# Hybrid decoder trunk in two layers: ScalarE issues first weights and three kinds of copies, and all blocks of x have rooms of their own

## The chip, the cores and the metric

The kernel runs on one core of one Trainium2 chip. The metric is the device time of one execution in microseconds (us); lower is better. TensorE (PE) multiplies matrices, VectorE (DVE) and ScalarE (ACT) work element by element, GpSimd (POOL) does so on SBUF alone, and SyncE (SP) issues DMA transfers. ScalarE can issue transfers too. Each engine works through its own instructions in order and waits on semaphores.

## The reference, cut to what matters

The input x has 1024 tokens of width 1024; 16 meta tokens are put ahead, so there are 1040 rows. Everything is float32. Each of the two layers computes

```python
u = rms_norm(h, norm_g)
dq, dk, dv, dz, fq, fk, fv, fz, f_logit = split(u @ w_in)    # w_in: 1024 x 4104
# 4 differential heads: two 64-wide query/key halves with rope, values of 128
p  = softmax(q1 k1' / 8) - lam * softmax(q2 k2' / 8)         # causal
o_a = rms_norm(p @ v_a, subln_g) * (1 - lambda_init)
# 8 forgetting heads of 64: cum = cumsum(log_sigmoid(f_logit + b_forget))
o_b = softmax(q_f k_f' / 8 + cum_q - cum_k) @ v_f            # causal
h = h + concat(o_a * silu(dz), o_b * silu(fz)) @ w_out
```

and a final RMS norm drops the meta rows.

## The kernel before, in words

**Split precision.** A float32 product is made of three float32r products: each operand is split into a high part (a rounded copy) and a low part (the rest), and high by high, low by high and high by low are added in PSUM. The normed and transposed input stands in two resident tiles, XTh (high) and XTl (low), with 1040 columns for the tokens.

**The start** (lines 936 to 968, then `prefetch` from line 969). Nine blocks of rows are loaded: block 0 is the 16 meta tokens, blocks 1 to 8 have 128 tokens each. `XORD` (line 38) gives the order of the loads: 1, 0, 2, 3, ..., 8. `htags` (line 944) gives each block a tag, which is a ring of buffers: block 0 and blocks 6 and 7 use "st" (three buffers), blocks 1 to 5 use "e" (four buffers, `NE`), block 8 uses "ot" (two, one of them for the norm's weights gb). With `W0` = 8 (line 39) the first weights, the key columns of unit 0, are loaded by `load_w` behind the ninth block. Then come three groups (`GRPS`, line 42): blocks 0 to 2, 3 to 5, 6 to 8. For each group `rms_stats` squares the blocks on ScalarE (line 256) and works out the inverse root on VectorE (lines 257 and 231 to 244). `rms_apply` makes u (line 267), and `put_ut` transposes it on TensorE (line 282), copies the high part on ScalarE (line 292) and subtracts the low part on VectorE (line 293).

**Weights.** `load_w` (line 296) loads 1024 x 128 weights in four transfers of 128 KB (lines 302 and 308) and splits each on GpSimd (lines 314 and 317). Raw and low parts share the tag "wlo" (six buffers). `prefetch(0, "qv")` (line 982) loads the first query columns into a free V buffer and the value columns of units 0 and 1 together, with the forget logits' columns, by `load_v01` (line 351, splits on lines 369 and 370).

**Units.** A layer has eight units of 128 columns: units 0 to 3 are the differential heads, units 4 to 7 pairs of forgetting (fox) heads. `unit_proj` (line 471) projects keys and queries in three chunks of columns by `proj` (line 333, matmuls on line 341). `CH_ALL` has chunks of 348, 346 and 346 columns, `CH_BLK` of 272, 384 and 384, whose borders are those of blocks. `CKB` is off, so `CH_ALL` is used for keys. In a differential unit the projection is copied out (line 491), its halves are exchanged by four small transfers (line 499), and the rope is worked out on VectorE and GpSimd (lines 500 to 502); then `split_k` and `split_q` make high parts on ScalarE (line 515 or 517) and low parts (line 508 or 510). The high part of the queries is duplicated into the other half of the partitions (line 560, two transfers per chunk or unit). In a fox unit the high keys are also copied (line 533) into a tile of tag "q2" with two buffers, beside rows of cumulated logits. Unit 0 projects the values of units 0 and 1 (`proj_v01`, line 373: meta rows on line 385, blocks on line 406) and the forget logits, which go to DRAM in eight small transfers (line 418). `attend` makes scores (lines 679 and 681), subtracts the maximum (line 685), exponentiates on ScalarE (line 692), transposes the probabilities (lines 854 to 870) and multiplies by the values.

**Order.** The helper `dma` (line 136) issues every transfer on SyncE. The program is written in the order above, but the framework lays out each engine's instructions anew by a simulated timeline (line 1168, `schedule_with_timeline_sim`): what is ready early in the simulation comes early, across stages. On the chip every engine, SyncE's queue too, then keeps its order.

Of the kernel before, what the change touches and what calls it, by code (L numbers as in the profile page):

```python
# [12 lines left out]
F32 = mybir.dt.float32  # L13
# [6 lines left out]
P = 128  # L20
NM = 16
SEQ = 1024
L = NM + SEQ
# [9 lines left out]
ST = 3  # L33
# [5 lines left out]
W0 = 8  # L39
# [34 lines left out]
CKB = False  # L74
# [4 lines left out]
WQ0 = False  # L79
WQ1 = False  # L80
# [33 lines left out]
def hybrid_kernel(ctx: ExitStack, tc: tile.TileContext, x, meta, norm_g, w_in, b_forget,  # L114
# [21 lines left out]
    def dma(dst, src):  # L136
        nc.sync.dma_start(out=f32(dst), in_=f32(src))  # L137

# [157 lines left out]
    def load_w(l, col, q=None, room=None, rawroom=None):  # L296
# [3 lines left out]
        for qt in range(4 if rawroom else 0):  # L300
            raws.append(rawroom(qt))
            (q or nc.sync).dma_start(out=raws[-1], in_=w_in[l, 256 * qt:256 * qt + 256, col:col + P].rearrange("(k p) c -> p k c", p=P))
# [30 lines left out]
    def proj(l, col, chunks, evac):  # L333
        his, los = ahead.pop((l, col), None) or load_w(l, col, nc.scalar if (WQ1 and l == 0 and col % 512 == 0 and col < 2048) else None)
# [38 lines left out]
    def proj_v01(l, his, los):  # L373
# [43 lines left out]
        for h in range(8):  # L417
            dma(fx[h, NM:].rearrange("(b t) -> b t", t=P), ft[8 * h:8 * h + 8])
# [52 lines left out]
    def unit_proj(l, j, U, tabs):  # L471
# [3 lines left out]
        ch_q = CH_ALL if l == 0 else CH_REAL  # L475
# [52 lines left out]
        yield from project(ck, CH_BLK if CKB and l == 0 and j == 0 else CH_ALL, 0, 1.0, split_k)  # L528
        if not diff and KE:
            U.Kb = []  # L530
            for m in range(2):
                k2 = q2t("k2")
                dma(k2[0:64], U.K1[m][halves[m]])
                dma(k2[64:68], augk[:, 2 * (j - 4) + m])
                U.Kb.append(k2[0:68])
# [12 lines left out]
        def split_q(src, c0, scale, t0, n):  # L548
# [10 lines left out]
            for m in range(2):  # L559
                dma(U.Qa[m][halves[1 - m], c], U.Qa[m][halves[m], c])  # L560
# [4 lines left out]
        if not diff and not KE:  # L565
            U.Kb = []
            for m in range(2):
                k2 = q2t("k2")
                dma(k2[0:64], U.K1[m][halves[m]])
# [374 lines left out]
    htags = [("st", ST)] + [("e", NE)] * 5 + [("st", ST)] * 2 + [("ot", OTB)]  # L944
    for i, b in enumerate(XORD):
        t0, n = blk(b)
        tg, nb = htags[b]
        hb = big.tile([P, L], F32, name="hb", tag=tg, bufs=nb or None)[:, :D]
# [5 lines left out]
        if i == W0:  # L954
            ck0 = unit_cols(0)[1]
            ahead[0, ck0] = load_w(0, ck0, nc.scalar if WQ0 else None, None, (lambda qt: wp.tile([P, 2, P], F32, name="wraw", tag="wlo", bufs=WLB or None)) if KR else None)
# [12 lines left out]
    def prefetch(l, todo):  # L969

        for w in todo:
# [3 lines left out]
            if w == "q":  # L975
                room = vp.tile([P, NB, 2, P], F32R, name="wroom", tag="V")
                ahead[l, col] = load_w(l, col, None, room,
                                       lambda qt: slot("es")[:, :256].rearrange("p (k c) -> p k c", k=2))
# [193 lines left out]
```

## Time and profile before

| what | value |
|---|---|
| three runs | 1501.41, 1500.04, 1497.89 us |
| median | 1500.04 us |
| the profiled execution | 1498.74 us |
| its span, first to last instruction | 1497.1 us |
| mean granted TensorE clock | 0.982 of full speed |
| TensorE busy | 1419.0 us, 95% |
| VectorE, ScalarE, GpSimd busy | 64%, 47%, 42% |

Times in the rows are from the span's start. A DMA's row tells when its engine issued it, not when the data moved; what waited for the data tells when it was there. In an idle remark, [25.62 <-DVE u L267] means that the engine stood still for 25.62 us and that VectorE's line 267 ended it. In a queue's row several issues can be merged into one ("x4"), and waiting between them is then inside the duration.

### The profile page before, as it was taken

Reading aid. Unit: us, or ns where it says so; the run is one execution under the profiler, and the core shown is the slowest. Engines: PE = TensorE matmul, PEld = TensorE weight load, DVE = VectorE, ACT = ScalarE, POOL = GpSimd, SP = SyncE. Lnnn points to the kernel's source line nnn. Section 1 sums busy time; section 2 is a strip of 40 time slices with the busy share of each in tenths; the row PEclk is TensorE's granted clock in tenths of the full one; section 3 lists DMA queues with packets and bytes.
Section 4 is the critical chain, followed back from the end, with each engine's and each line's share of the span. In section 5 each row is a group of like instructions: output and inputs, shape, how many; then the busy total and the mean of one; then the engine's idle time right before and its main releaser. Section 6 shows DMA issues by size and latency. Waiting matters only on the chain.

```text
span 1497.1 us, 26781 instructions
## 1 busy us (share of the span) xinstructions
PE 1419.0 (95%) x9262; PEld 1348.8 (90%) x9262; DVE 955.3 (64%) x2721; ACT 699.9 (47%) x1729; POOL 627.8 (42%) x1118
## 2 busy tenths in 40 slices
PE   2889989899999999999999899899999999999997
PEld 2888989899999999997789899899999999999886
DVE  3548695957665656566564498867757555755653
ACT  3335554445454555456222365545445555654521
POOL 3525553633344444565106255435334454445500
PEclk7899999999999999999999999999999999999999
DMA  8314331332234224346434044224242323243632
GB/s 192 56 40 63 50 73 32 82 30 55 59 86 76 52 52 75 73 154 183 103 128 94 20 63 68 47 51 75 34 79 63 79 45 78 61 108 88 220 120 91
DMA packets 112280, 119.63 MB, mean 80 GB/s; under 512 B 15441, under 2 KB 92881, under 8 KB 112145
## 3 DMA queue, kind: packets, MB, share of 16 engines
q1 hardware_dynamic: 112144, 117.93, 36.2%
q8 instruction: 73, 1.20, 0.3%
q14 instruction: 63, 0.51, 0.1%
HBM read 70.92 MB, written 21.54 MB: 62 GB/s over the span
## 4 chain that ended last, share of the span: by engine, by line
PE 75%; DVE 8%; DMA 5%; SPq 4%; ACT 3%; issue 2%; POOL 2%; DVEq 0%; POOLq 0%; ACTq 0%
PE pj L341 36%; PE pss L1059 5%; PE pj L1059 5%; PE pss L679 4%; PE pt L854 4%; PE pss L681 4%; SPq L137 3%; PE pj L406 2%; PE po L788 2%; PE po L789 2%; DMA sw<-raw 2%; DMA wraw<-in_w_in_dram 2%; DVE E L685 2%; PE pt L1059 1%; POOL sw L501 1%
## 5 line engine op out<-in xcount | busy, mean ns | idle before, releaser
L341 PE MATMUL pj<-XTh,whi 128*128 128x346 f32 (+5 forms) x1392 | 454.7, 328 | 7.6 <-POOL whi L314 3.9
L341 PE MATMUL pj<-XTh,wlo 128*128 128x346 f32 (+5 forms) x1392 | 451.2, 325 | 3.6 <-POOL wlo L317 3.5
L341 PE MATMUL pj<-XTl,whi 128*128 128x346 f32 (+5 forms) x1392 | 450.4, 324 | 0.0
L341 PEld LDWEIGHTS pj<-XTh,whi 128*128 128x128 f32 x1392 | 263.0, 189 | 12.2 <-POOL whi L314 5.9
L341 PEld LDWEIGHTS pj<-XTh,wlo 128*128 128x128 f32 x1392 | 263.6, 189 | 6.2 <-POOL wlo L317 5.7
L341 PEld LDWEIGHTS pj<-XTl,whi 128*128 128x128 f32 x1392 | 263.3, 189 | 0.7 <-DVE XTl L293 0.3
L685 DVE CUSTOM_DVE_ANT_0 E<-pss,cst 128x456 f32<-128x456 f32 (+6 forms) x384 | 210.2, 557 | 68.6 <-PE pss L681 42.1
L692 ACT ACTIVATE E<-E,cst 128x400 f32<-128x400 f32 (+2 forms) x192 | 172.4, 898 | 137.2 <-DVE cst L685 130.5
L317 POOL TENSOR_TENSOR wlo<-wraw,whi 128x256 fp32r<-128x256 f32 x232 | 183.3, 790 | 65.7 <-PE pj L341 50.9
L763 DVE TENSOR_TENSOR ptl<-pt,pth 128x512 fp32r<-128x512 f32 (+1 forms) x240 | 150.2, 634 | 54.9 <-ACT pth L762 51.1
L314 POOL TENSOR_SCALAR whi<-wraw 128x256 fp32r<-128x256 f32 x232 | 106.7, 460 | 186.7 <-DMA wraw<-in_w_in_dram 156.6
L762 ACT CAST pth<-pt 128x512 fp32r<-128x512 f32 (+1 forms) x240 | 126.9, 543 | 92.9 <-PE pt L854 34.5
L679 PE MATMUL pss<-k,qa 128*128 128x400 f32 (+7 forms) x448 | 152.4, 345 | 10.0 <-DMA qa<-qa 5.0
L709 POOL TENSOR_SCALAR E<-E,cst 128x400 f32<-128x400 f32 (+2 forms) x96 | 83.8, 874 | 132.3 <-DVE cst L708 102.3
L662 POOL TENSOR_SCALAR XTl<-ql 64x128 fp32r<-64x128 f32 x136 | 50.8, 379 | 120.4 <-PE pss L681 95.6
L679 PEld LDWEIGHTS pss<-k,qa 128*128 128x128 f32 x448 | 85.0, 190 | 15.7 <-DVE cst L685 9.3
L854 PE MATMUL pt<-cst,E 128*128 128x128 f32 x576 | 88.0, 275 | 0.2
L788 PE MATMUL po<-pth,V 128*128 128x256 f32 x320 | 85.0, 286 | 0.0
L789 PE MATMUL po<-ptl,V 128*128 128x256 f32 x320 | 82.8, 287 | 0.0
L501 POOL TENSOR_TENSOR sw<-sw,sin 128x694 f32<-128x694 f32 (+3 forms) x32 | 51.0, 1595 | 57.2 <-DMA sw<-raw 51.4
L681 PE MATMUL pss<-k,XTl 128*128 128x400 f32 (+6 forms) x224 | 72.0, 327 | 0.0
L681 PE MATMUL pss<-k,q 68*128 68x400 f32 (+6 forms) x224 | 71.9, 325 | 0.0
(300 smaller groups left out, 2948.7 us busy)
## 6 DMA issues: line engine op xcount, KB each, us to landing
wraw<-in_w_in_dram SPq DMA_DIRECT2D x248, 128.0 KB
hb<-in_x_dram SPq DMA_DIRECT2D x16, 512.0 KB
wor<-in_w_out_dram SPq DMA_DIRECT2D x64, 128.0 KB
sw<-raw SPq DMA_DIRECT2D x48, 86.8 KB
ms<-OT SPq DMA_DIRECT2D x8, 520.0 KB
k<-k SPq DMA_DIRECT2D x16, 260.0 KB
h<-hb SPq DMA_DIRECT2D x8, 512.0 KB
ms<-OT SPq DMA_DIRECT2D x8, 512.0 KB
```

The lines of the kernel that those rows point to most:

```text
L317: nc.gpsimd.tensor_tensor(out=lo, in0=raw, in1=hi.bitcast(F32), op=ALU.subtract)
L341: nc.tensor.matmul(ps[:, :n], lhsT=w, rhs=xx[:, k, t0:t0 + n], start=(cnt == 0), stop=(cnt == 23))
L679: nc.tensor.matmul(ps[:, :nn], lhsT=U.Qa[m][:, t:t + P], rhs=U.K1[m][:, c0:c0 + nn], start=True, stop=False)
L681: nc.tensor.matmul(ps[:, :nn], lhsT=low[m], rhs=U.Kb[m][:, c0:c0 + nn], start=False, stop=True)
L685: nc.vector.tensor_tensor_reduce(out=E[:, c0:c0 + n], in0=ps[:, :n], in1=k, scale=-1.0, scalar=s[:, c - 1:c] if CHN and c else -NEG, op0=A ...
L692: nc.scalar.activation(E[:, :W], E[:, :W], AF.Exp, scale=-1.0, bias=lo, accum_out=s[:, 4:5])
L762: nc.scalar.copy(hi, ps)
L763: nc.vector.tensor_tensor(out=lo, in0=ps, in1=hi.bitcast(F32), op=ALU.subtract)
L788: nc.tensor.matmul(o[:, :256], lhsT=U.V[:, kb, hd, :], rhs=hi, start=False, stop=False)
L789: nc.tensor.matmul(o[:, :256], lhsT=U.V[:, kb, hd, :], rhs=lo, start=False, stop=last)
L854: nc.tensor.transpose(ps[:, (2 * a + b) * P:(2 * a + b + 1) * P], PP[:, k0:k0 + P], ident)
L1059: nc.tensor.matmul(ps, lhsT=xx[:, k, m0:m0 + P], rhs=wo[k][w][:, c], start=(k == 0 and i == 0), stop=(k == KT - 1 and i == 2))
```

## The change

Five things change. The first weights (keys of unit 0) are loaded right behind the first block of x instead of behind the ninth, and both they and the first query weights are issued by ScalarE, in two transfers of 256 KB into one tile of tag "qa0" or "qa1" instead of four of 128 KB. Block 5 of x gets a buffer of tag "k1" and block 8 one of "k0". Unit 0 uses the chunks `CH_BLK` for its keys in both layers and for its queries in layer 0. The duplicates of queries, the copies of fox keys and the transfers of the forget logits are issued by ScalarE (`dma_a`). The rope's exchanges, the low queries, the rows of logits and all other weights stay with SyncE.

```diff
--- before.py
+++ after.py
@@ -36,7 +36,7 @@
 MW = 584
 AHEAD = 3
 XORD = (1, 0, 2, 3, 4, 5, 6, 7, 8)
-W0 = 8
+W0 = 0
 ON_POOL = ()
 SPL_POOL = ()
 GRPS = ((0, 1, 2), (3, 4, 5), (6, 7, 8))
@@ -71,13 +71,13 @@
 SH = 0
 PP = ()
 WARM = 20
-CKB = False
+CKB = (0,)
 KR = True
 PG = ()
 AQ = True
 AV = True
-WQ0 = False
-WQ1 = False
+WQ0 = True
+WQ1 = True
 CORD = (1, 0, 2, 3)
 PSB = (0, 0, 0, 0)
 Z_AT = {0: [0], 1: [1], 2: [2], 4: [3], 7: [4, 5, 6, 7]}
@@ -135,6 +135,10 @@
 
     def dma(dst, src):
         nc.sync.dma_start(out=f32(dst), in_=f32(src))
+
+    def dma_a(dst, src):
+
+        nc.scalar.dma_start(out=f32(dst), in_=f32(src))
 
     def pj(nm="pj"):
         return ps_j.tile([P, 512], F32, name=nm, tag="pj")
@@ -293,13 +297,20 @@
                 nc.vector.tensor_tensor(out=lv, in0=psv, in1=hv.bitcast(F32), op=ALU.subtract)
 
 
-    def load_w(l, col, q=None, room=None, rawroom=None):
+    def load_w(l, col, q=None, room=None, rawroom=None, rawtag=None):
 
         his, los = [], []
         raws = []
-        for qt in range(4 if rawroom else 0):
-            raws.append(rawroom(qt))
-            (q or nc.sync).dma_start(out=raws[-1], in_=w_in[l, 256 * qt:256 * qt + 256, col:col + P].rearrange("(k p) c -> p k c", p=P))
+        if rawroom == "half":
+
+            whole = stk.tile([P, L], F32, name="wraw4", tag=rawtag, bufs=STB or None)[:, :D].rearrange("p (k c) -> p k c", k=KT)
+            for a in (0, 4):
+                (q or nc.sync).dma_start(out=whole[:, a:a + 4], in_=w_in[l, P * a:P * a + 4 * P, col:col + P].rearrange("(k p) c -> p k c", p=P))
+            raws = [whole[:, 2 * qt:2 * qt + 2] for qt in range(4)]
+        elif rawroom:
+            for qt in range(4):
+                raws.append(rawroom(qt))
+                (q or nc.sync).dma_start(out=raws[-1], in_=w_in[l, 256 * qt:256 * qt + 256, col:col + P].rearrange("(k p) c -> p k c", p=P))
         for qt in range(4):
           if rawroom:
             raw = raws[qt]
@@ -331,7 +342,7 @@
             late.pop(0)()
 
     def proj(l, col, chunks, evac):
-        his, los = ahead.pop((l, col), None) or load_w(l, col, nc.scalar if (WQ1 and l == 0 and col % 512 == 0 and col < 2048) else None)
+        his, los = ahead.pop((l, col), None) or load_w(l, col)
         for t0, n in chunks:
             ps = pj(f"pj_{l}_{col}")
             cnt = 0
@@ -415,7 +426,7 @@
         ft = ptp.tile([P, 256], F32, name="ft", tag="pm")[0:64, 0:P]
         nc.scalar.copy(ft, ps[0:64, 0:P])
         for h in range(8):
-            dma(fx[h, NM:].rearrange("(b t) -> b t", t=P), ft[8 * h:8 * h + 8])
+            dma_a(fx[h, NM:].rearrange("(b t) -> b t", t=P), ft[8 * h:8 * h + 8])
 
 
     def forget(l):
@@ -472,7 +483,7 @@
         diff = j < 4
         cq, ck, cv, _ = unit_cols(j)
         tq = 0 if l == 0 else NM
-        ch_q = CH_ALL if l == 0 else CH_REAL
+        ch_q = (CH_BLK if j in CKB else CH_ALL) if l == 0 else CH_REAL
         U.diff, U.j, U.l, U.tq = diff, j, l, tq
         lowhalf, tophalf = slice(0, 64), slice(64, 128)
         halves = (lowhalf, tophalf)
@@ -525,12 +536,12 @@
                 hi = U.K1[m][halves[m], t0:t0 + n]
                 hi_part(hi, x, scale)
                 sub(U.K1[m][halves[1 - m], t0:t0 + n], x, scale, hi, f'k{m}')
-        yield from project(ck, CH_BLK if CKB and l == 0 and j == 0 else CH_ALL, 0, 1.0, split_k)
+        yield from project(ck, CH_BLK if j in CKB else CH_ALL, 0, 1.0, split_k)
         if not diff and KE:
             U.Kb = []
             for m in range(2):
                 k2 = q2t("k2")
-                dma(k2[0:64], U.K1[m][halves[m]])
+                dma_a(k2[0:64], U.K1[m][halves[m]])
                 dma(k2[64:68], augk[:, 2 * (j - 4) + m])
                 U.Kb.append(k2[0:68])
         U.Qa = [stk.tile([P, L], F32R, name=f"qa{m}") for m in range(2)]
@@ -557,7 +568,7 @@
             c = slice(todo_q[0][0], t0 + n)
             todo_q.clear()
             for m in range(2):
-                dma(U.Qa[m][halves[1 - m], c], U.Qa[m][halves[m], c])
+                dma_a(U.Qa[m][halves[1 - m], c], U.Qa[m][halves[m], c])
             if not diff:
                 for m in range(2):
                     dma(q2s[m][0:64, c], ql[halves[m], c])
@@ -566,7 +577,7 @@
             U.Kb = []
             for m in range(2):
                 k2 = q2t("k2")
-                dma(k2[0:64], U.K1[m][halves[m]])
+                dma_a(k2[0:64], U.K1[m][halves[m]])
                 dma(k2[64:68], augk[:, 2 * (j - 4) + m])
                 U.Kb.append(k2[0:68])
 
@@ -941,11 +952,11 @@
     dma(bfb, bcast_rows(b_forget, P))
     hbs = {}
     gb = None
-    htags = [("st", ST)] + [("e", NE)] * 5 + [("st", ST)] * 2 + [("ot", OTB)]
+    htags = [("st", ST)] + [("e", NE)] * 4 + [("k1", STB)] + [("st", ST)] * 2 + [("k0", STB)]
     for i, b in enumerate(XORD):
         t0, n = blk(b)
         tg, nb = htags[b]
-        hb = big.tile([P, L], F32, name="hb", tag=tg, bufs=nb or None)[:, :D]
+        hb = (stk if tg[0] == "k" else big).tile([P, L], F32, name="hb", tag=tg, bufs=nb or None)[:, :D]
         dma(hb[:n], meta if b == 0 else x2[P * (b - 1):P * b])
         hbs[b] = (hb, n)
         if i == 0:
@@ -953,7 +964,7 @@
             dma(gb, bcast_rows(norm_g[0], P))
         if i == W0:
             ck0 = unit_cols(0)[1]
-            ahead[0, ck0] = load_w(0, ck0, nc.scalar if WQ0 else None, None, (lambda qt: wp.tile([P, 2, P], F32, name="wraw", tag="wlo", bufs=WLB or None)) if KR else None)
+            ahead[0, ck0] = load_w(0, ck0, nc.scalar if WQ0 else None, None, "half", "qa0")
     utags = ("k0", "k1", "qa0", "qa1") * 2 + ("ql",)
     for grp in GRPS:
         us = [stk.tile([P, L], F32, name="u", tag=utags[b])[:, :D] for b in grp]
@@ -974,8 +985,11 @@
                 ahead[l, col] = load_w(l, col)
             if w == "q":
                 room = vp.tile([P, NB, 2, P], F32R, name="wroom", tag="V")
-                ahead[l, col] = load_w(l, col, None, room,
-                                       lambda qt: slot("es")[:, :256].rearrange("p (k c) -> p k c", k=2))
+                if l == 0:
+                    ahead[l, col] = load_w(l, col, nc.scalar if WQ1 else None, room, "half", "qa1")
+                else:
+                    ahead[l, col] = load_w(l, col, None, room,
+                                           lambda qt: slot("es")[:, :256].rearrange("p (k c) -> p k c", k=2))
             if w == "v":
                 ahead[l, "v"] = load_v01(l)
```

## Rows read from the trace of the kernel before

**Rows 1.** The page: busy time by engine; the chain that ended last, by engine.

```profile
PE 1419.0 (95%) x9262; PEld 1348.8 (90%) x9262; DVE 955.3 (64%) x2721; ACT 699.9 (47%) x1729; POOL 627.8 (42%) x1118
...
PE 75%; DVE 8%; DMA 5%; SPq 4%; ACT 3%; issue 2%; POOL 2%; DVEq 0%; POOLq 0%; ACTq 0%
```

**Rows 2.** TensorE's waits, whole span: line, who released it, us in total, times, longest us.

```profile
PE pt L282 <- DVE u L267: 29.0, 3, 25.6
PE pss L799 <- DMA qa<-qa: 5.9, 1, 5.9
PE pss L679 <- DMA qa<-qa: 5.0, 2, 4.8
```

**Rows 3.** Timeline of TensorE, 10 to 88 us: start us, us, instruction [idle before <- releaser].

```profile
13.22 3.61 PE L282 MATMUL pt<-cst,u 128*128 128x128 f32 x16 [0.53 <-DVE u L267]
...
42.45 2.82 PE L282 MATMUL pt<-cst,u 128*128 128x128 f32 x12 [25.62 <-DVE u L267]
...
73.17 0.28 PE L385 MATMUL pj<-vwh,mm 128*48 128x264 f32 x1
...
87.03 0.35 PE L799 MATMUL pss<-k,qa 128*128 128x16 f32 x1 [5.91 <-DMA qa<-qa]
```

**Rows 4.** Timeline of VectorE, 0 to 62 us: the three groups' norms.

```profile
10.69 3.67 DVE L267 SCALAR_TENSOR_TENSOR u<-hb,cst,gb 16x1024 f32<-16x1024 f32 x3
...
20.82 3.81 DVE L267 SCALAR_TENSOR_TENSOR u<-hb,cst,gb 128x1024 f32<-128x1024 f32 x3
...
41.11 4.15 DVE L267 SCALAR_TENSOR_TENSOR u<-hb,cst,gb 128x1024 f32<-128x1024 f32 x3
```

**Rows 5.** Timeline of ScalarE, 0 to 62 us: the eighth and the ninth block's squares.

```profile
15.96 1.06 ACT L256 ACTIVATE u<-hb 128x1024 f32<-128x1024 f32 x1
...
37.75 1.06 ACT L256 ACTIVATE u<-hb 128x1024 f32<-128x1024 f32 x1 [19.19 <-DMA hb<-in_x_dram]
```

**Rows 6.** Timeline of SyncE's queue, 0 to 62 us: DMA issues.

```profile
6.88 4.82 SPq L137 DMA_DIRECT2D gsc<-in_subln_g_dram  x1
11.74 4.72 SPq L302 DMA_DIRECT2D wraw<-in_w_in_dram  x4
16.50 8.72 SPq L302 DMA_DIRECT2D cst<-in_w_in_dram  x4
25.27 0.86 SPq L137 DMA_DIRECT2D cos<-in_rope_cos_dram  x1
...
28.09 2.75 SPq L137 DMA_DIRECT2D bfb<-in_b_forget_dram  x1
30.97 0.61 SPq L137 DMA_DIRECT2D hb<-in_x_dram  x1
```

**Rows 7.** Groups of instructions, shapes apart: a block's low parts, busy us, mean ns.

```profile
L293 DVE TENSOR_TENSOR XTl<-pt,XTh 128x512 fp32r<-128x512 f32 x32 | 21.3, 685 | 10.9 <-ACT XTh L292 10.6
```

**Rows 8.** Timeline of GpSimd, 0 to 75 us: weight splits.

```profile
20.15 0.43 POOL L314 TENSOR_SCALAR whi<-wraw 128x256 fp32r<-128x256 f32 x1 [16.21 <-DMA wraw<-in_w_in_dram]
...
42.57 3.28 POOL L370 TENSOR_TENSOR vwl<-wraw,vwh 128x256 fp32r<-128x256 f32 x2 [3.48 <-DVE u L267]
...
57.58 0.74 POOL L370 TENSOR_TENSOR vwl<-wraw,vwh 128x256 fp32r<-128x256 f32 x1
```

**Rows 9.** Three stretches: length, busy us by engine, granted clock, DMA share, GB/s.

```profile
2.00:14.00 12.00, 7.98 (x52) 7.70 (x53) 5.09 (x14) 7.17 (x16) 1.91 (x8) 0.97 1.00 352
14.00:26.00 12.00, 2.83 (x14) 2.49 (x12) 8.77 (x24) 4.52 (x10) 3.82 (x5) 0.64 0.95 43
26.00:38.00 12.00, 0.00 (x0) 0.00 (x0) 0.00 (x0) 0.25 (x1) 6.49 (x12) 0.50 0.83 202
```

**Rows 10.** DMA issues of the copies: count, ns min/median/max, first and last start us.

```profile
L137 SPq DMA_DIRECT2D qa<-qa x48: 461/500/1239, 83.6 to 1309.3; - x48
...
L137 SPq DMA_DIRECT2D k<-k x16: 461/467/468, 353.9 to 1301.6; - x16
```

**Rows 11.** SyncE's queue, whole span: waits for the scores' second matmul.

```profile
SPq L137 <- PE pss L681: 101.4, 11, 15.7
```

## The prediction

> **What bounds the kernel now.** I read the page's busy times first, then TensorE's waits, then the timelines of the first 110 us engine by engine. TensorE is busy 95% of the span [rows 1], so a change counts only where TensorE stands still, or where it makes TensorE stand still. Its waits name few such places [rows 2]: one of 25.6 us before the transposes of line 282, one of 5.9 us before line 799 and 5.0 us in two waits before line 679, the last three for the copy of query halves (qa<-qa). The reader should see that a third of its idle time, 78 us, is one wait at the start.
>
> That wait is from 16.83 us (13.22 + 3.61), when the transposes of blocks 1, 0 and 2 end, to 42.45 us [rows 3]. VectorE applies the norm three times at 10.69, three times at 20.82 and three times at 41.11 us [rows 4]. ScalarE squares eight blocks up to 17.02 us; the ninth waits 19.19 us for its transfer and comes at 37.75 us [rows 5]. SyncE's queue shows why: one x transfer is issued at 30.97 us, behind gsc, four weight issues of k, four of q (from 16.50), the rope tables and the biases [rows 6]. By the code it is block 5, the fifth tile on a tag with four buffers. Its group (3, 4, 5) comes before (6, 7, 8) in TensorE's order, so the norms finished at 24.63 us lie idle until 42.45 us. From there TensorE is never without work up to 81.12 us: six blocks' transposes and the projections of k and q end at 73.17 us, 30.72 us after 42.45, and the v projection follows [rows 3].
>
> **The change part by part.** The sum is made against the profiled execution, 1498.74 us (span 1497.1 and 1.6 around it), 1.3 below the median of 1500.04.
>
> *Rooms for all x.* Block 5 gets a buffer of k1 and block 8 one of k0; nothing must be freed, so all nine issues stand at the head of SyncE's queue. What is late next is VectorE. Group 0 is applied by 14.36 us. Its subtractions (line 293) take four of 0.685 us [rows 7] and the small meta ones, 3.0 us. Each further group needs its statistics, 2.3 us (ScalarE's square ends at 38.81, the applies start at 41.11 [rows 4, 5]), 3.8 us of applies and six subtractions, 4.1 us: 10.2 us. So the last block is split at 14.4 + 3.0 + 10.2 + 10.2 = 37.8 us.
>
> *First weights in ScalarE's queue, and chunks at block borders.* With a first k chunk of 272 columns TensorE needs only blocks 0 to 2 and can begin at 17.4 us (14.4 + 3.0) instead of after group 1. From there the work that took 30.72 us before ends at 48.1 us, if nothing starves it. By VectorE the bound is much the same: after 37.8 us the last chunk of k and of q remains, 384 of 1040 columns, at most that share of the 30.72 us (which hold transposes too), 11.3 us: 49.1 at most. The v projection then starts at 48.1 instead of 73.17: **25.1 us saved**. The first weights must be split by 17.4 us: issued at 2 to 3 us, they share the engines with x; GpSimd, waiting 16.21 us up to 20.15 [rows 8], splits them in under 5 us. This is hidden.
>
> The price is that 1.05 MB of k and q weights now move among the x transfers. From 2 to 14 us the engines are fully busy at 352 GB/s [rows 9]: more queues cannot move more. At that rate the weights delay x by 3.0 us, at the 43 GB/s of 14 to 26 us (weights among gsc's tiny pieces) by 24 us. I take the row between, 202 GB/s at 0.83 busy, 243 when full, as it too mixes weights and long rows: 4.3 us. The eighth block was read at 15.96 us, so the last of nine is there at 15.96 + 1.5 + 4.3 = 21.8; VectorE turns to its statistics at 27.6, after 3.2 us of squares. So it costs 0, and up to 17.5 us at the slow rate. The Trainium skill ("DMA: Bandwidth & Descriptors", Issuing engines are not separate DMA queues) speaks against this part: a second issuing engine shares the same 16 DMA engines and saves issue time alone. By that rule the queue itself gives no bandwidth, and what is left is the earlier place; the sum above counts only that.
>
> *Weights of v.* Their last split ended at 58.32 us (57.58 + 0.74) [rows 8]; before, TensorE wanted them 15 us later, now it would want them 10 us earlier. SyncE loses the eight issues from 11.74 to 25.2 us (13.4 us), and the wait of 3.48 us behind a late norm goes, so the end can be 41.4 us; the other end is 58.3. I take 45, nearer the first because the issues are gone from that queue by the diff: no cost, at most 10.2 us.
>
> *Copies begun by ScalarE.* Moved from SyncE: 48 query copies of 0.5 us, 16 fox-key copies of 0.47 us [rows 10] and 16 forget-logit transfers, at most as long: 40 us. What an issue holds ScalarE for is not in the trace: 0 to 0.5 us each. The chain has 3% ScalarE, 45 us of its 699.9 busy [rows 1], so 6.4% of its time counts: **2.6 us lost** of 40 (ends 0 and 40). Behind an issue stand the exponentials and PSUM copies of attention, and TensorE's transposes wait for them; mostly it has projection matmuls to do meanwhile. The logits' eight issues per layer stand ahead of attention's first exponentials. SyncE is relieved by the same 40 us, which can shorten the three waits for qa<-qa by 0 to 10.9 us; I take 0, since those copies left SyncE as soon as ScalarE had written the halves, and the wait is mostly the flight. They therefore stay.
>
> *Fox keys.* A copy's room (two buffers) is free only when the unit before has made its last scores. On SyncE such waits for line 681 sum to 101.4 us in 11 [rows 11]. On ScalarE the same wait would hold everything queued behind it. Ends 0 and 101.4; I take 0, as each engine's order is laid out by simulated readiness, so that other ready ScalarE work stands ahead. The chunk borders in layer 1 move no column: 0.
>
> Sum: 1498.74 - 25.1 + 2.6 = 1476.2; beside the median, which lies 1.3 higher, **1477**.
>
> **The rivals.** (1) *The v weights stay late*: v starts at 58.3, saving 14.9 us: 1498.74 - 14.9 + 2.6 = 1486.4. For it: two of them at a time go through two buffers, and the engines are full early. Against: 13.4 us less in the queue ahead. Chance 0.17. (2) *The query waits go too*: 10.9 more: 1465.3, and 1462.7 if ScalarE's issues cost nothing. For it: SyncE's queue is shorter. Against: those waits are flight. Chance 0.09. (3) *ScalarE stands at the key copies*: the 11 waits of 9.2 us move to it, and half reaches TensorE: 1476.2 + 50.7 = 1526.9. It decides the sign once 22.5 us, 2.0 per wait, reach TensorE. Against: the layout by readiness. Chance 0.07. (4) *The order is laid out such that block 5 or the first weights are late again*: the change does not do what it says, 1498.74 + 2.6 = 1501.3. Against: nothing has to be freed for them. Chance 0.05. The forecast, from 1470 to 1484, keeps 0.62.
>
> **How the numbers follow.** The time is that of the forecast. The range goes down to rival 2 (1463) and up over rival 1 with twice ScalarE's cost (1486.4 + 2.6 = 1489); rivals 3 and 4 lie outside. About 0.2%, 3 us, is what a measurement can tell from no change. Faster: forecast and rivals 1 and 2, 0.88. Same: most of rival 4, 0.04. Slower: rival 3 and the rest, 0.08.
>
> **What would show it.** Right: x issues all before 7 us; no TensorE wait above some 5 us at line 282; first k matmul before 22 us; VectorE's last split in the start near 38 us; the v projection (line 385) starting near 48 us; the later stages about 25 us earlier with ScalarE's copies taking near 0.5 us each. Wrong: line 385 waiting for GpSimd (rival 1); long ScalarE idle times just before k<-k that end with line 681 (rival 3); an x transfer far down a queue (rival 4); or attention of units 1 to 3 longer than before, which would mean that an order laid out anew gives back what the start won.

## The result, and the profile after

The changed kernel takes **1487.76 us** (median of five runs, 1486.78 to 1492.38) against 1501.31 for the kernel before on the same chip: ratio 0.9919, 95% interval 0.99 to 0.9939. It is faster, by 11.5 us between the two profiled executions (span 1485.6 against 1497.1), where 22.5 were forecast. In the changed kernel line numbers of the start are 4 higher (L286 is L282 of before), those of the projections 11 (L352, L396, L810 are L341, L385, L799).

The page's busy times and chain hardly moved against [rows 1]:

```profile
PE 1416.9 (95%) x9262; PEld 1350.0 (91%) x9262; DVE 958.7 (65%) x2721; ACT 698.6 (47%) x1729; POOL 619.2 (42%) x1118
...
PE 75%; DVE 7%; DMA 4%; ACT 2%; issue 2%; SPq 1%; POOL 1%; DVEq 0%; ACTq 0%; POOLq 0%
```

TensorE's waits after (line, releaser, us in total, times, longest), beside [rows 2]:

```profile
PE pt L286 <- DVE u L271: 16.1, 2, 15.9
...
PE pss L690 <- DMA qa<-qa: 4.7, 2, 3.8
PE pss L810 <- ACT V L421: 3.9, 1, 3.9
PE pt L286 <- DVE XTl L297: 3.4, 1, 3.4
```

The wait of 25.6 us for block 5 is gone, and one of 15.9 us for the *first* norm stands in its place. TensorE's timeline (start us, us, instruction, idle before and its releaser) says where:

```profile
24.86 1.03 PE L286 MATMUL pt<-cst,u 16*128 16x16 f32 x8 [15.95 <-DVE u L271]
...
31.06 0.36 PE L352 MATMUL pj<-XTh,whi 128*128 128x272 f32 x1 [1.33 <-ACT XTh L296]
...
42.90 0.66 PE L286 MATMUL pt<-cst,u 128*128 128x128 f32 x4 [3.44 <-DVE XTl L297]
...
67.98 0.28 PE L396 MATMUL pj<-vwh,mm 128*48 128x264 f32 x1
```

The v projection starts at 67.98: 5.2 us earlier than the 73.17 of [rows 3], and 20 us later than the forecast's 48.1. The transposes, which began at 12.02 before, begin at 24.86. What is late is x. The timeline of ScalarE, its queue included:

```profile
0.80 1.03 ACTq L308 DMA_DIRECT2D wraw<-in_w_in_dram  x2
...
4.94 1.06 ACT L260 ACTIVATE u<-hb 128x1024 f32<-128x1024 f32 x1 [1.57 <-DMA hb<-in_x_dram]
...
18.03 1.06 ACT L260 ACTIVATE u<-hb 16x1024 f32<-16x1024 f32 x1 [11.94 <-DMA hb<-in_meta_tokens_dram]
```

The first weights' two transfers are issued at 0.80 us together with the first x; the meta block, issued by SyncE at 1.71, is squared only at 18.03. SyncE's queue:

```profile
1.71 0.43 SPq L137 DMA_DIRECT2D hb<-in_meta_tokens_dram  x1
2.19 3.95 SPq L137 DMA_DIRECT2D hb<-in_x_dram  x1
6.17 2.00 SPq L137 DMA_DIRECT2D gb<-in_norm_g_dram  x1
8.22 9.81 SPq L137 DMA_DIRECT2D hb<-in_x_dram  x5
18.07 0.45 SPq L137 DMA_DIRECT2D cst<-in_w_in_dram  x1
```

One x issue takes 3.95 us and five take 9.81, where rooms_only below needs 0.42 and 3.41. All nine x stand at the queue's head as foretold, but the queue itself is held. The first 24 us in two stretches (length, busy us by engine, clock, DMA share, GB/s):

```profile
2.00:14.00 12.00, 6.32 (x40) 6.13 (x40) 0.00 (x0) 2.51 (x4) 4.06 (x12) 0.95 0.99 121
14.00:26.00 12.00, 1.03 (x8) 0.92 (x8) 4.25 (x14) 7.03 (x14) 2.15 (x4) 0.50 1.01 320
```

In [rows 9] the first stretch moved 352 GB/s; now, as fully busy, it moves 121, and the only weights among x are the 0.5 MB of k: the q weights, from 27.1 us on, come behind x. The second half of the first k weights was ready for GpSimd at 17.76 us; from 14 us to then the rate is 171 GB/s, from then to 26 us it is 387. VectorE's last low part of the start ends at 53.57 us (51.68 + 1.89), not at 37.8.

**Where the 11.5 us came from.** I weighed every matmul by the usual interval from its start to the next, by shape, in the trace of before, and compared when equal shares of that work are done (us against before; minus is earlier):

| share of TensorE's work | 3% | 6% | 10% | 20% | 56% | 60% | all |
|---|---|---|---|---|---|---|---|
| before, at us | 79.9 | 130.4 | 191.6 | 352.3 | 866.9 | 926.5 | 1488.2 |
| after | -5.2 | -8.3 | -3.8 | -14.0 | -20.7 | -15.9 | -11.7 |
| rooms_only | -8.2 | -12.2 | -12.2 | -12.8 | -14.8 | -15.6 | -14.7 |
| rooms_fx | -8.5 | -12.4 | -5.1 | -5.4 | -4.3 | -2.9 | -1.4 |
| k_as_before | -10.8 | -9.1 | +4.8 | -1.7 | +1.1 | +3.6 | +3.4 |
| k_fx_back | -13.6 | -13.6 | -6.2 | -17.5 | -20.6 | -18.9 | -21.3 |
| rooms_chunks_qa | -15.0 | -14.9 | -7.7 | -16.5 | -24.3 | -23.0 | -23.5 |

The start had won 8.3 us at 6% of the work, of 25.1 forecast. What followed lost 4.5, won 16.9 and lost 9.0 again, in stretches where the diff moves only issues. Both needed an explanation: the *start* that came short, and the order *behind* it.

### The profile page after: what moved, and what is told of

It reads as the page before. It is cut to its first block, busy times and chain, and to the rows that moved or that the text cites. A ratio compares the mean times of both kernels' runs of the same rounds, so it can differ in the third digit from the quotient of the medians.

```text
span 1485.6 us, 26706 instructions
## 1 busy us (share of the span) xinstructions
PE 1416.9 (95%) x9262; PEld 1350.0 (91%) x9262; DVE 958.7 (65%) x2721; ACT 698.6 (47%) x1729; POOL 619.2 (42%) x1118
## 4 chain that ended last, share of the span: by engine, by line
PE 75%; DVE 7%; DMA 4%; ACT 2%; issue 2%; SPq 1%; POOL 1%; DVEq 0%; ACTq 0%; POOLq 0%
PE pj L352 36%; PE pss L1073 5%; PE pj L1073 5%; PE pss L690 4%; PE pss L692 4%; PE pt L865 4%; PE po L800 3%; PE pj L417 3%; PE po L799 2%; DMA sw<-raw 1%; SPq L137 1%; DVE E L696 1%; PE pt L1073 1%; DVE raw L511 1%; DMA mt<-ms 1%
## 5 line engine op out<-in xcount | busy, mean ns | idle before, releaser
L352 PE MATMUL pj<-XTh,whi 128*128 128x346 f32 (+5 forms) x1392 | 453.8, 328 | 5.0 <-ACT XTh L296 1.9
L352 PE MATMUL pj<-XTh,wlo 128*128 128x346 f32 (+5 forms) x1392 | 452.9, 326 | 1.2 <-POOL wlo L328 1.2
L352 PE MATMUL pj<-XTl,whi 128*128 128x346 f32 (+5 forms) x1392 | 451.8, 325 | 1.1 <-DVE XTl L297 1.1
L352 PEld LDWEIGHTS pj<-XTh,whi 128*128 128x128 f32 x1392 | 264.3, 190 | 9.0 <-POOL whi L325 1.9
L352 PEld LDWEIGHTS pj<-XTh,wlo 128*128 128x128 f32 x1392 | 265.1, 190 | 2.5 <-POOL wlo L328 1.8
L352 PEld LDWEIGHTS pj<-XTl,whi 128*128 128x128 f32 x1392 | 264.8, 190 | 2.3 <-DVE XTl L297 1.7
L696 DVE CUSTOM_DVE_ANT_0 E<-pss,cst 128x346 f32<-128x346 f32 (+6 forms) x384 | 212.0, 558 | 77.0 <-PE pss L692 61.7
L703 ACT ACTIVATE E<-E,cst 128x656 f32<-128x656 f32 (+3 forms) x192 | 172.5, 898 | 141.7 <-DVE cst L696 137.8
L773 ACT CAST pth<-pt 128x512 fp32r<-128x512 f32 (+1 forms) x240 | 123.3, 545 | 72.8 <-PE pt L865 30.9
L325 POOL TENSOR_SCALAR whi<-wraw 128x256 fp32r<-128x256 f32 x232 | 101.0, 436 | 116.4 <-DMA wraw<-in_w_in_dram 115.2
L690 PEld LDWEIGHTS pss<-k,qa 128*128 128x128 f32 x448 | 84.8, 190 | 16.9 <-DVE cst L696 9.7
L799 PE MATMUL po<-pth,V 128*128 128x256 f32 x320 | 82.7, 283 | 0.0
L512 POOL TENSOR_TENSOR sw<-sw,sin 128x694 f32<-128x694 f32 (+5 forms) x32 | 50.6, 1581 | 76.0 <-DMA sw<-raw 63.8
```

Source lines behind the costliest of these rows:

```text
L352: nc.tensor.matmul(ps[:, :n], lhsT=w, rhs=xx[:, k, t0:t0 + n], start=(cnt == 0), stop=(cnt == 23))
L690: nc.tensor.matmul(ps[:, :nn], lhsT=U.Qa[m][:, t:t + P], rhs=U.K1[m][:, c0:c0 + nn], start=True, stop=False)
L696: nc.vector.tensor_tensor_reduce(out=E[:, c0:c0 + n], in0=ps[:, :n], in1=k, scale=-1.0, scalar=s[:, c - 1:c] if CHN and c else -NEG, op0=A ...
L703: nc.scalar.activation(E[:, :W], E[:, :W], AF.Exp, scale=-1.0, bias=lo, accum_out=s[:, 4:5])
L773: nc.scalar.copy(hi, ps)
L799: nc.tensor.matmul(o[:, :256], lhsT=U.V[:, kb, hd, :], rhs=hi, start=False, stop=False)
```

## The experiments

Theory: **crowding**. The first weights, at the head of a second queue, take the transfers' turns from x. Rivals: the weights' place costs nothing, as the prediction had it, and something else limits the start; or ScalarE's issues cost what was missing. 

**rooms_only: before + rooms, nothing else.**

```diff
-    htags = [("st", ST)] + [("e", NE)] * 5 + [("st", ST)] * 2 + [("ot", OTB)]
+    htags = [("st", ST)] + [("e", NE)] * 4 + [("k1", STB)] + [("st", ST)] * 2 + [("k0", STB)]
...
-        hb = big.tile([P, L], F32, name="hb", tag=tg, bufs=nb or None)[:, :D]
+        hb = (stk if tg[0] == "k" else big).tile([P, L], F32, name="hb", tag=tg, bufs=nb or None)[:, :D]
```

> The kernel before with the rooms of blocks 5 and 8 alone; all weights stay in SyncE's queue, four transfers each, now behind the last x. Crowding theory (the first weights, issued ahead of x, hold x back, and that ate the gain): x is whole by about 17 us as before, the last split on VectorE comes near 40 us, the v projection starts at 55 to 60 us instead of 73.2, and the time is 1481 to 1487 us, below that of the full change. Rival (the start was worth only what the full change gave, whatever the order of the transfers): v starts near 68 us, and the time is 1490 us or more.

1484.27 us, ratio 0.9898 (0.988 to 0.9916). The rooms alone give at least the whole gain of the change (the two intervals overlap). The time is the one that crowding expected, but the start is only part of the way: the v projection starts at 65.02 us, not at 55 to 60, and VectorE's last low part ends at 51.09, not near 40. The first stretch:

```profile
2.00:14.00 12.00, 9.16 (x56) 8.84 (x56) 5.20 (x14) 7.27 (x17) 1.90 (x8) 1.00 0.97 367
```

**copies_back: the change with its copies on SyncE.**

```diff
     def dma_a(dst, src):
-        nc.scalar.dma_start(out=f32(dst), in_=f32(src))
+        nc.sync.dma_start(out=f32(dst), in_=f32(src))
```

> The full change with the query copies, fox-key copies and logit transfers issued by SyncE again. Crowding theory: the start is the same as with the full change (v at 68 us, plus or minus 1) and the time is within 3 us of its 1487.8. Rival (the copies on ScalarE give back some 9 us in layer 1, where units 0 to 7 took 556 us instead of 547): 1478 to 1481 us.

1492.97 us, ratio 0.9953 (0.9934 to 0.9971): within the change the copies on ScalarE are worth about 5 us (the intervals just touch). Both expectations missed. The v projection starts at 71.91 us, not at 68, so some 4 of the 5 us are lost before the first of the moved copies (74.97 us in the changed kernel) is issued at all.

**copies_only: before + the copies on ScalarE** (three kinds of lines, four places).

```diff
-            dma(fx[h, NM:].rearrange("(b t) -> b t", t=P), ft[8 * h:8 * h + 8])
+            dma_a(fx[h, NM:].rearrange("(b t) -> b t", t=P), ft[8 * h:8 * h + 8])
...
-                dma(k2[0:64], U.K1[m][halves[m]])
+                dma_a(k2[0:64], U.K1[m][halves[m]])
...
-                dma(U.Qa[m][halves[1 - m], c], U.Qa[m][halves[m], c])
+                dma_a(U.Qa[m][halves[1 - m], c], U.Qa[m][halves[m], c])
```

> The kernel before with the three kinds of copies on ScalarE alone. Crowding theory: the start is that of before (wait of 25.6 us, v at 73 us), and the time is within 3 us of before. Rival (the copies on ScalarE cost): 3 to 10 us slower than before.

1519.38 us, ratio 1.0123 (1.0105 to 1.0141). The same edit costs 18 us here, more than either expectation allowed. A price of the issues themselves cannot be 18 us here and nothing, or less, within the change.

**probe_loads: single loads, one after the other**, each waited for by a small VectorE copy (the stamp); nothing of the model is computed.

```python
    for l, col in ((0, 512), (0, 512), (0, 0), (1, 512), (1, 0)):
        w_halves(l, col)
        stamp(T[:, :, 0])
```

> Nothing of the model is computed: single loads, each waiting for the one before, their ends stamped by VectorE. In order: two blocks of x alone; the first k weights (0.5 MB in rows of 512 B, two transfers); the same again; the q columns; two column groups of layer 1; another group as four transfers; the logits' columns (rows of 32 B); the norm's gains (4 B); then two blocks of x beside a weight load. If 512 B rows are slow as such, every weight load takes about 12 us (43 GB/s). If only the first touch of those rows is slow, the first of layer 0 and the first of layer 1 take about 12 us and the others 3 to 5 us. If neither, all take 3 to 5 us, and x beside weights takes as long as alone plus that.

An x block (0.5 MB, rows of 4 KB) took 3.5 us from issue to VectorE's stamp. The first k weights (0.5 MB, rows of 512 bytes) took 6.6 us, and 6.5 when read again; the query columns of unit 0 took 11.2 and 11.6 in the two layers, another group 7.2, one in four transfers instead of two 6.8, the logits' columns (rows of 32 bytes) 9.3. None of the three expectations holds whole: rows of 512 bytes are slow, a first reading is not slower than a second, and why the query columns are the slowest stays open. With weights issued between two x blocks, the second x took 7.5 us instead of 3.5. So weights are slow by themselves, and they slow x beside them. Two stretches in which weights alone are under way (length, busy us of VectorE and GpSimd, clock, DMA share, GB/s):

```profile
8.00:14.60 6.60, 0.10 (x1) 0.00 (x0) 1.00 0.31 79
15.00:21.00 6.00, 0.00 (x0) 0.00 (x0) 1.00 0.34 87
```

**rooms_wfirst: rooms_only + first k weights at the head of ScalarE's queue.** All but 32 of TensorE's 9262 matmuls stand at the same place of its order as in rooms_only.

```diff
-W0 = 8
+W0 = 0
-WQ0 = False
+WQ0 = True
```

> The kernel before with the rooms for blocks 5 and 8, and with one thing more: the four transfers of the first k weights stand at the head of ScalarE's queue instead of behind x on SyncE's. The order on the engines is else nearly that of rooms_only (1484.27 us; first statistics on VectorE at 8.4 us, TensorE's first norm transposes at 11.9, v projection from 67.0). Crowding: the weights hold x back as in the changed kernel; first statistics at 14 to 21 us, v projection from 70 or later, time 1487 to 1495. Rival, the price that the prediction took (weights among x cost nothing): statistics before 10 us, v projection at 67.0 or earlier, time 1481 to 1485.

1492.61 us, ratio 0.9956 (0.9941 to 0.9971): **8.3 us slower** than rooms_only, with the signs of the changed kernel. SyncE's queue, the first stretch, and TensorE (the "v projection from 67.0" of the expectations is its second part, line 406; by line 385 rooms_only starts it at 65.02):

```profile
2.19 2.06 SPq L137 DMA_DIRECT2D hb<-in_x_dram  x1
7.36 0.33 SPq L137 DMA_DIRECT2D gb<-in_norm_g_dram  x1
7.73 9.42 SPq L137 DMA_DIRECT2D hb<-in_x_dram  x5
```

```profile
2.00:14.00 12.00, 6.72 (x40) 6.53 (x40) 0.82 (x5) 4.11 (x8) 4.17 (x12) 0.98 1.00 147
```

```profile
21.61 1.03 PE L282 MATMUL pt<-cst,u 16*128 16x16 f32 x8 [12.30 <-DVE u L267]
...
70.19 0.28 PE L385 MATMUL pj<-vwh,mm 128*48 128x264 f32 x1
```

367 GB/s become 147 by one edit, the first transposes move from 11.92 to 21.61 us, the v projection by 5.2 us. The first statistics come at 13.04 us instead of 8.42, a little before the 14 to 21 expected; the first norm then waits 4.53 us more for gb, the norm's weights, which stand in the held queue too. Crowding is shown; the rival falls.

The DMA view tells what the engines' time went to (queue, packets, MB, share of 16 engines): from 2 to 14 us q10, ScalarE's queue with the weights, and q1, SyncE's with x; last, the weights alone in probe_loads, from 8.00 to 14.60 us.

```profile
q10 hardware_dynamic: 853, 0.41, 68.2%
q1 hardware_dynamic: 379, 1.36, 32.2%
```

```profile
q10 hardware_dynamic: 1056, 0.52, 31.2%
```

By my estimate from these lines (share times 16 engines times the stretch, by packets) a packet of weights, of 0.5 KB, took 154 ns beside x and 31 ns alone, and a packet of x, of 3.6 KB, took 163 ns. Beside x a short packet cost the engines as much time as a long one.

**k_as_before: the change with its first k weights on SyncE behind all x.**

```diff
-load_w(0, ck0, nc.scalar if WQ0 else None, None, "half", "qa0")
+load_w(0, ck0, None, None, lambda qt: wp.tile([P, 2, P], F32, name="wraw", tag="wlo", bufs=WLB or None))
```

> The changed kernel (1487.76 us, v projection from 68.0) with the first k weights loaded as before: four transfers on SyncE behind all x, in their old rooms. Copies on ScalarE, chunk borders and q weights are those of the change. Crowding: first statistics at 8 to 9 us instead of 21.4, first k matmul near 22 us, v projection from 50 to 62, time 1470 to 1482 (6 to 18 less, unless the order laid out anew gives some back later). Rival, the weights' place costs nothing: statistics still near 21, v projection within 2 us of 68.0, time 1485 to 1490.

1502.84 us, ratio 1.0026 (1.0015 to 1.0037). The start behaves as crowding says (first norm at 10.40 us instead of 23.53, first k matmul at 24.07, v projection at 62.40 instead of 67.98), yet the time misses: the whole is 15 us slower. By the table it loses 14 between 6% and 10% of the work; that stretch is taken up below.

**rooms_chunks: rooms_only + unit 0's chunk borders.**

```diff
-CKB = False
+CKB = (0,)
...
-        ch_q = CH_ALL if l == 0 else CH_REAL
+        ch_q = (CH_BLK if j in CKB else CH_ALL) if l == 0 else CH_REAL
...
-        yield from project(ck, CH_BLK if CKB and l == 0 and j == 0 else CH_ALL, 0, 1.0, split_k)
+        yield from project(ck, CH_BLK if j in CKB else CH_ALL, 0, 1.0, split_k)
```

> The kernel before with the rooms for blocks 5 and 8 and the chunk borders of unit 0 at block borders, nothing else (no copies on ScalarE, weights on SyncE behind x). If the chunk borders are worth what the prediction put in them (TensorE begins with blocks 0 to 2 alone): first k matmul at 18 to 20 us instead of 22.3, v projection 3 to 10 us earlier than 67.0, time 1474 to 1481. Rival, x and the weights of v, not the borders, set the start: v projection at 65 to 69, time 1482 to 1487.

1483.71 us, ratio 0.9894 (0.988 to 0.9909): not to be told from rooms_only. First k matmul 18.20 us instead of 22.32, v projection 59.02 instead of 65.02; but TensorE then waits 4.1 us instead of 1.8 at line 799 for qa<-qa, and the first scores come 3.7 us earlier, not 6. The start came as the first expectation had it, the time as its rival had it.

**rooms_copies: rooms_only + all copies on ScalarE** (the diffs of rooms_only and copies_only together).

> The kernel before with the rooms for blocks 5 and 8 and the copies of queries, fox keys and logits begun by ScalarE. If the copies have a price of their own on ScalarE: 1484.3 plus the 18.1 us that they cost alone, 1500 to 1504. If it is the order laid out anew that made 18 us (the copies alone) or minus 5 us (within the change), the sign does not carry over: anything from 1475 to 1496, with the difference to rooms_only in the units of layer 0 and layer 1, not in the start. The prediction's own term would give 1486.9.

1496.53 us, ratio 0.998 (0.9966 to 0.9993), 12.3 us over rooms_only. So I took the copies apart.

**rooms_fx, rooms_fxpool, rooms_qa, rooms_k: rooms_only + one kind each.** The logits' 16 transfers by ScalarE; the same by GpSimd; the query copies by ScalarE; the fox keys by ScalarE. Each takes its lines of the diff of copies_only; rooms_fxpool is

```diff
-            dma(fx[h, NM:].rearrange("(b t) -> b t", t=P), ft[8 * h:8 * h + 8])
+            nc.gpsimd.dma_start(out=f32(fx[h, NM:].rearrange("(b t) -> b t", t=P)), in_=f32(ft[8 * h:8 * h + 8]))
```

> rooms_only (1484.27 us) with one third of the copies' change: the 16 transfers of 4 KB with the forget logits are begun by ScalarE. All three together cost 12.3 us there (rooms_copies, 1496.53). By the issues' own price, 16 of at most 0.5 us on ScalarE, at most 8 us and more likely under 1: 1484 to 1486. If the order laid out anew makes the difference, these few small transfers move the time like the others: 1478 to 1496, in the same stretch (130 to 200 us) as in rooms_copies.

> rooms_only with the same 16 transfers of the logits begun by GpSimd instead of by ScalarE: ScalarE issues nothing, the order on the engines changes in about as many places as in rooms_fx. If a price of ScalarE's issues is what costs time, this one stays at rooms_only's 1484.3 within 2 us whatever rooms_fx does. If it is the order laid out anew, it moves as far as rooms_fx does, in either direction.

> rooms_only with the second third: the 48 copies of query halves are begun by ScalarE. By the prediction's terms: at most 24 us on ScalarE, 6.4% of it on the path, 1.5 us, and the query waits unchanged: 1484 to 1487. Rival 2 of the prediction (SyncE's shorter queue ends the query waits): 1475 to 1481. Order laid out anew: anywhere from 1478 to 1497.

> rooms_only with the last third: the 16 fox-key copies are begun by ScalarE. If ScalarE stands at them (rival 3 of the prediction), ScalarE shows idle times ended by line 679's scores or a DMA just before its key copies, and the time rises by 5 us or more: 1490 to 1500. If they find their rooms free by then, as the prediction took: 1483 to 1487 and no such idle times.

| | us | ratio to before | against rooms_only |
|---|---|---|---|
| rooms_fx | 1497.70 | 0.9979 (0.997 to 0.9988) | +13.4 |
| rooms_fxpool | 1491.50 | 0.9938 (0.9924 to 0.9953) | +7.2 |
| rooms_qa | 1478.21 | 0.9857 (0.9839 to 0.9875) | -6.1 |
| rooms_k | 1487.31 | 0.9913 (0.9899 to 0.9928) | +3.0, the intervals overlap |

By the ratios, each to the kernel before on the same chip, the differences are +12, +6, -6 and +2 us. The whole loss of rooms_copies sits in 16 transfers of 4 KB, and about half of it comes without ScalarE issuing anything. The transfers themselves are at the same place: the first of unit 0's eight starts at 100.78 us on SyncE in rooms_only and at 100.83 on ScalarE in rooms_fx, the eighth ends at 103.46 and 104.56. What moved in rooms_fx is their *reading back* for the forget gate, which SyncE issues in both. SyncE's queue in rooms_only, then in rooms_fx:

```profile
128.74 0.41 SPq L137 DMA_DIRECT2D cst<-fx  x1
```

```profile
129.91 2.42 SPq L137 DMA_DIRECT2D sw<-raw  x4
...
134.76 1.29 SPq L137 DMA_DIRECT2D qa<-qa  x2
...
138.74 0.35 SPq L137 DMA_DIRECT2D cst<-fx  x1
```

The order laid out anew has put the gate's reading 10.0 us later, behind four sw and two query copies; in k_as_before it is at 139.54, in the changed kernel at 140.52. With it moves the gate on ScalarE, which loads two function tables. ScalarE in k_as_before:

```profile
147.15 1.28 ACT L455 ACT_TABLE_LOAD   x1
148.45 0.26 ACT L455 ACTIVATE cst<-cst 128x65 f32<-128x65 f32 x1
148.72 1.28 ACT L658 ACT_TABLE_LOAD   x1
...
150.97 0.48 ACT L742 ACTIVATE sq<-po 128x128 f32<-128x128 f32 x2
```

Both loads now stand ahead of squares for which TensorE waits, and a low clock follows (TensorE's timeline; three stretches):

```profile
151.33 0.58 PE L760 MATMUL pt<-XTl,sq 128*128 128x1 f32 x2 [4.74 <-ACT sq L742]
```

```profile
140.00:150.00 10.00, 6.57 (x41) 5.93 (x39) 8.55 (x19) 6.39 (x12) 7.40 (x14) 1.00 0.66 85
150.00:160.00 10.00, 8.67 (x40) 8.61 (x41) 5.66 (x18) 4.25 (x12) 1.64 (x3) 0.66 0.05 12
160.00:170.00 10.00, 10.00 (x72) 9.97 (x71) 5.02 (x14) 4.23 (x10) 2.54 (x7) 1.00 0.01 2
```

In rooms_fx the same wait is 3.32 us; in rooms_only one table load stands before those squares and one behind (136.74 and 138.92 us), and TensorE does not stop there. In the changed kernel the reading is as late, but the squares stand ahead of both loads, and TensorE has no wait over 1.6 us there. ScalarE in the changed kernel:

```profile
146.88 0.45 ACT L742 ACTIVATE sq<-po 128x128 f32<-128x128 f32 x2
...
147.35 1.28 ACT L455 ACT_TABLE_LOAD   x1
...
148.92 1.28 ACT L658 ACT_TABLE_LOAD   x1
```

This place does not explain everything. By the table rooms_fx is 7.4 us behind rooms_only at 20% of the work and 13.3 at the end, so some 6 us are lost elsewhere. And in rooms_fxpool, which loses 7.2 us, the reading back has not moved:

```profile
128.40 0.35 SPq L137 DMA_DIRECT2D cst<-fx  x1
```

Weighed in the same way, rooms_fxpool is some 2.5 us behind rooms_only at 20% of the work and 8.8 at the end; the cause of its loss is not shown.

**fx_back, k_fx_back, rooms_chunks_qa.** The change with the logits' transfers on SyncE; the same with the edit of k_as_before too; and rooms + the chunk borders of rooms_chunks + the query copies of rooms_qa. The edit of fx_back:

```diff
-            dma_a(fx[h, NM:].rearrange("(b t) -> b t", t=P), ft[8 * h:8 * h + 8])
+            dma(fx[h, NM:].rearrange("(b t) -> b t", t=P), ft[8 * h:8 * h + 8])
```

> The changed kernel (1487.76 us) with one part undone: the 16 transfers of the forget logits are issued by SyncE again. If they have a price of their own on ScalarE, the 13.4 us of rooms_fx come back: 1473 to 1478. If that was the order laid out anew, the sign is open here: anything from 1478 to 1500, the difference again in stretches where nothing was edited.

> The changed kernel with two parts undone: first k weights on SyncE behind x (as in k_as_before, 1502.84 us) and the logits' transfers on SyncE. If the logits' transfers were what k_as_before lost between its v projection (64 us) and 200 us: that loss of 14 us is gone, 1483 to 1490, and with the earlier start it beats the changed kernel. If the order at large is the cause, no such thing follows: 1478 to 1505.

> The parts that gained by themselves, together: rooms (1484.27 us), chunk borders (0.6 less), query copies on ScalarE (6.1 less); first weights, fox keys and logits as before. If the parts add: 1476 to 1479, the fastest so far or level with rooms_qa (1478.21). If the order laid out anew decides: 1472 to 1492.

fx_back: 1484.80 us, 0.9904 (0.9887 to 0.9921), 3.0 under the change with intervals that overlap. There the gate's reading moves from 140.52 to 135.19 us, but the changed kernel had no wait over 1.6 us at this place: little to win, and the 13.4 us do not carry over. k_fx_back: **1477.35**, 0.9849 (0.9835 to 0.9864): with the logits back, the first weights behind x are worth 7.5 us against fx_back, as rooms_wfirst said (8.3), and 25.5 us are won against k_as_before, more than the 14 expected. rooms_chunks_qa: **1475.32**, 0.9834 (0.982 to 0.9848), the fastest median here, 24.7 under before (its interval overlaps those of k_fx_back and rooms_qa); the parts add up within 2.3 us. Its start, by TensorE:

```profile
18.36 0.56 PE L341 MATMUL pj<-XTh,whi 128*128 128x272 f32 x1 [0.78 <-ACT XTh L292]
21.92 0.59 PE L341 MATMUL pj<-XTh,wlo 128*128 128x272 f32 x1 [3.00 <-POOL wlo L317]
...
58.13 0.28 PE L385 MATMUL pj<-vwh,mm 128*48 128x264 f32 x1
...
72.18 0.35 PE L799 MATMUL pss<-k,qa 128*128 128x16 f32 x1 [6.10 <-DMA qa<-qa]
```

```profile
10.00:20.00 10.00, 5.20 (x25) 4.41 (x25) 8.45 (x24) 7.91 (x18) 0.60 (x2) 0.64 1.03 238
20.00:30.00 10.00, 6.68 (x29) 6.36 (x30) 6.58 (x9) 1.17 (x2) 8.73 (x13) 0.50 1.01 134
30.00:40.00 10.00, 8.49 (x59) 7.73 (x58) 9.90 (x20) 3.98 (x8) 6.22 (x10) 1.00 0.61 135
```

## Why the prediction was right in direction and wrong in size

**Rooms for all x: right.** No x waits for a room, the 25.6 us wait went, and rooms_only shows that this carries the gain. Forecast and result agree in sign.

**The price of the first weights among x: the step that failed.** The prediction worked out 3.0 us at 352 GB/s and 24 at 43, took 4.3 for 1.05 MB, and let the slack of the last x hide it (by its own figures 2.6 us: 27.6 less 3.2 of squares, less 21.8): "costs 0, and up to 17.5 us at the slow rate". The slow end was nearer, for half the bytes. The stretch ran at 121 GB/s with only the 0.5 MB of k in it; the last x was issued by 18.03 us, not before 7; the meta block came at 18.0 us and TensorE began its transposes at 24.86 instead of 12.02. In rooms_wfirst the last five x issues end at 17.15 us, against 6.53 in rooms_only, and the place of the k weights costs 8.3 us of the whole; k_fx_back prices it at 7.5. Two errors lie in it. The row at 43 GB/s was put down to gsc's tiny pieces, but weights alone run at 79 to 87 GB/s (probe_loads), far from the 243 that the sum took. And the slack was reckoned for the *last* x block, while the weights, issued first, delay the first group, on which everything hangs. The prediction's sentence on the Trainium skill ("DMA: Bandwidth & Descriptors", Issuing engines are not separate DMA queues: transfers begun by several engines interleave on the same 16 and save issue time alone) was right as far as it went, and I drew too little from it. The same page of the Trainium skill (Queues, rings and completion order) says that each DMA engine takes turns between the queues it has work for, packet by packet; that agrees with x and weights both creeping while the DMA share is 0.99, and these runs cannot show the turns themselves.

**"If nothing starves it": the second part of the same sum.** Even with the weights behind x, rooms_chunks_qa begins at 18.36 us, 1 us from the 17.4 forecast, but starts the v projection at 58.13, not 48.1. TensorE waits for the first weights' splits (3.00 us and smaller), and its granted clock is 0.50 (1.2 of 2.4 GHz) from 20 to 30 us, behind waits of 3.76 and 3.00 us, where the 30.72 us taken as the work had run at 0.92 on the mean. What it won was then paid in part at the first scores: the query wait, which the prediction expected to stay at 5.9, is 1.8 when v starts at 65.02 (rooms_only), 4.1 at 59.02 (rooms_chunks) and 6.1 at 58.13; it does not follow the start alone, being 8.2 in k_as_before at 62.40. What is late next after x is the query copy: in rooms_chunks_qa TensorE stands still from 66.08 us, and the first copy is issued at 67.18.

**Weights of v late (rival 1): not seen**, for v never came early enough. Its time, 1486.4, is near the result by accident. **Rival 4** is half true: the first weights were not late, but they made x late.

**Copies on ScalarE, +2.6.** The issues are as cheap as thought: 48 queries and 16 fox keys of 0.47, 16 logits of 0.31, 35 us in all, and ScalarE's busy time is unchanged. But the term was the wrong kind of term. The same edits are worth about -5 us within the change, +12 with rooms alone and +18 by themselves. The prediction named what fits these signs, "an order laid out anew", only in the last line of what could be wrong. It should have carried 10 us of range by itself.

**Fox keys, 0: right.** rooms_k is 3.0 us up with overlapping intervals. ScalarE stands still before one key copy that line 681 releases, at 1290.18 us, for 1.9 us inside an idle time of 2.97 that TensorE's line 870 ends, so the copy itself costs nothing there. Rival 3 falls. The query copies gained 6.1 us, but not at the waits of rival 2: those of line 679 are 4.2 us in rooms_only, 6.7 in rooms_qa (whose profiled execution, 1484.38 us, was the slowest of its five) and 4.3 in rooms_chunks_qa.

**What stays open:** why the order puts the gate's reading 10 us later when ScalarE issues the logits' transfers was not tried, and the rest of the losses of rooms_fx and rooms_fxpool is not explained. Nor is what the query copies gain: in the table the four kernels that have them on ScalarE win 6.5 to 11.3 us between 10% and 20% of the work, after losing 4.5 to 13.9 between 6% and 10%; the two that do not (rooms_only and rooms_fx) win under 1 us there. For the losses of the changed kernel behind 56% of the work I have equal-work times, and no cause shown. And the first weights early, but on SyncE's own queue, were not tried, so the second queue's part in the crowding is not parted from that of the early place.

## What to carry to other kernels

Ask of a load that is moved ahead not only how many bytes it adds but at what rate its own shape runs, and who stands behind it in *every* queue: the first block's delay counts, not only the last one's. Price an issue moved to another engine by what the laid-out order does with everything that depends on it; where a planner lays out the order, move one kind at a time and measure each. Of this change the rooms and the query copies gained by themselves, and the chunk borders alone could not be told from nothing; the three together take 1475.3 us instead of 1487.8.

## What the runs showed that I had not expected

0.5 MB in rows of 512 bytes takes 6.5 to 11.6 us by itself (0.31 and 0.34 DMA share in the two stretches shown), against 3.5 us in rows of 4 KB; a second reading is no faster. Beside x the share is full and the whole rate falls from 367 to 147 GB/s: a load that leaves the engines mostly idle when alone fills them when it shares. The queue of the *other* engine feels it too: an x issue on SyncE went from 0.42 to 3.95 us while ScalarE's two weight issues took 1.03 together.
